# One level of the gated scores in a hybrid decoder layer: 16 by 16 products and ScalarE copies, or one product with 128 fixed columns and a masked copy

## The chip, the cores and the metric

The kernel runs on one core of one Trainium2 chip. The metric is the device time of one execution in microseconds (us). The core has TensorE for matrix products (its results land in PSUM), VectorE and ScalarE for elementwise work and for bringing results out of PSUM, GpSimd for further elementwise work, and SyncE, which issues most DMA transfers.

## The reference

One layer of a decoder runs for a prompt of 2048 tokens and for 8 samples of 8 tokens, with the same weights. After a norm comes one input projection; its columns feed four retention heads and four gated heads (HGRN2), all with 128 keys and 128 values. Their outputs are normed, gated, projected and added to the input; a squared-ReLU feed-forward layer follows. The part that matters here is the score matrix of the gated heads:

```python
def step(S, inp):                                  # one chunk of tokens
    qb, kb, vb, gb = inp                           # gb = log of the forget gate
    b = jnp.cumsum(gb, axis=2)
    diff = b[:, :, :, None, :] - b[:, :, None, :, :]
    decay = jnp.exp(jnp.where(causal[:, :, None], diff, -jnp.inf))
    A = jnp.einsum('bhtd,bhsd,bhtsd->bhts', qb, kb, decay)
    o = jnp.einsum('bhts,bhsv->bhtv', A, vb) + jnp.einsum('bhtd,bhdv->bhtv', qb * jnp.exp(b), S)
    ...
```

The decay between two tokens differs for each of the 128 key channels, so `A` is not one plain product of queries and keys.

## The kernel before, in words

The 2112 tokens are cut into three token groups: 640 prompt tokens, 768 prompt tokens, and 64 sample tokens with the last 640 prompt tokens. The kernel first does the mixing of each group (input projection, heads, output projection), then the feed-forward layer of each. Weights are streamed from memory; ScalarE and VectorE cut each into two parts, `hi` and `lo` (lines 273 and 287), and a projection multiplies three combinations of parts. These long runs of matmuls (`proj`, line 344; `values`, line 751; line 1214 in the feed-forward layer) make up most of the stream of TensorE.

**Order of the work.** `proj` and `values` call `tick()` as they go: in `proj` once for each weight and part, that is after two matmuls (one for each half of the tokens). Small work of the heads is hung on an agenda with `at(tick, function)`, and is emitted when the tick comes, so it stands between the matmuls of the projection of the next head. `mixer` fills the agenda for one head pair; ticks in this text are counted from its start. The order of emission is the order on TensorE; on the other engines the framework may move an instruction that it takes to be waiting behind others.

**The levels.** A chunk has C = 128 tokens. Its 128 by 128 score matrix, kept transposed (keys by queries) in `AT`, is put together by levels: for w in `LEVELS = (64, 32, 16, 8, 4, 2)` the tokens are cut into blocks of 2w, and the level gives the scores of the second w queries of each block with its first w keys. `exponents`, `decays` and `decayed` make a slab `x["qk", w]`, in which the first half of each block holds keys times the decay up to the middle of the block and the second half holds queries times the decay from there. A product of the two halves is then the wanted score. Level w = 16 is the one of 32 tokens.

A group has five or six chunks, split into two segments `g.segs`: two and three chunks in the first and the third group, three and three in the second. A level is done once for each segment `sg`, in one of three ways, chosen in `level` (line 1015):
- `kept` (line 911): for each chunk one matmul with the whole chunk, 128 columns, as fixed operand (weights) and all second halves, 64 columns, as moving operand (line 923). The result holds scores of all keys; VectorE's masked copy (`copy_predicated`, line 924) brings the wanted ones into `AT`.
- `corners` (line 971): for each chunk and each block one matmul with w fixed and w moving columns (line 980). ScalarE copies the results to their place in `AT`, one copy for each block position and all chunks of the segment (line 983).
- `quad` (line 999): the last level in another way.

All matmuls on `qk` are in fp32. Results go to PSUM banks of a pool of four, `pm` (tiles named `mm` and `po`), which all small work of the heads shares.

**Other work near this level.** `turn` (ticks 60 and 64 for the two segments) transposes keys on TensorE (line 853), and ScalarE brings them out (855 or 857). `own` (ticks 67 and 70) makes the diagonal of `AT` by sums over channels (lines 512 and 513) and a masked copy (944). `gates` and `project` take the finished projections out of PSUM (650) and apply the sigmoid on ScalarE (364, with a table load; the table for exponentials is loaded back at 366). Level w = 32 comes at ticks 52 and 55, level w = 8 at 73 and 76, each before the edit. The outputs read `AT` only after all levels (line 1103).

Of the kernel before, what the change touches and what calls it, by code (L numbers as in the profile page):

```python
# [202 lines left out]
class Kernel:  # L203
# [5 lines left out]
    def at(self, when, fn, *a):  # L209
        heapq.heappush(self.agenda, (when, self.n_at, fn, a))  # L210
        self.n_at += 1
# [651 lines left out]
    def mixer(self, g, p, b, t0):  # L863
# [9 lines left out]
        at = lambda t, fn, *a: self.at(t0 + t, fn, *a)  # L873
# [37 lines left out]
        def kept(i, qk, sg):  # L911

            w = LEVELS[i]
            second = lambda t: t.rearrange("p (n h m) -> p n h m", h=2, m=w)[:, :, 1]
            if sg == 2:
                ps = self.mm(NS // 2).rearrange("p (n m) -> p n m", m=w)
                nc.tensor.matmul(ps, qk[:, :P], second(qk[:, :NS]), start=True, stop=True)
                nc.vector.copy_predicated(second(self.ATs[:, :NS]), second(msk[:, NLV + i, :NS]), ps)
                return
            seg, m = g.segs[sg], len(g.segs[sg])  # L920
            ps = self.mm(m * P // 2).rearrange("p (c n m) -> p c n m", c=m, m=w)
            for j, c in enumerate(seg):
                nc.tensor.matmul(ps[:, j], qk[:, cols[c]], second(qk[:, cols[c]]), start=True, stop=True)  # L923
            nc.vector.copy_predicated(self.AT[sg][:, :m].rearrange("p c (n h m) -> p c n h m", h=2, m=w)[:, :, :, 1],
                                      second(msk[:, i]).unsqueeze(1).to_broadcast([P, m, P // (2 * w), w]), ps)
# [45 lines left out]
        def corners(w, sg):  # L971

            nb = P // (2 * w)
            seg, m = g.segs[sg], len(g.segs[sg])
            qk = x["qk", w]
            ps = self.mm(m * nb * w)
            for j, c in enumerate(seg):
                for r in range(nb):
                    s0 = cols[c].start + 2 * w * r
                    nc.tensor.matmul(ps[0:w, (r * m + j) * w:(r * m + j + 1) * w], qk[:, s0:s0 + w], qk[:, s0 + w:s0 + 2 * w],  # L980
                                     start=True, stop=True)
            for r in range(nb):
                nc.scalar.copy(self.AT[sg][2 * w * r:2 * w * r + w, :m, 2 * w * r + w:2 * w * (r + 1)],
                               ps[0:w, r * m * w:(r + 1) * m * w].rearrange("p (c t) -> p c t", t=w))
# [14 lines left out]
        def quad(sg):  # L999
            seg, m = g.segs[sg], len(g.segs[sg])  # L1000
            a, e = self.seg_cols(g, seg)
            s0 = cols[seg[0]].start
            second = lambda t: t.rearrange("p (n h i) -> p n h i", h=2, i=2)[:, :, 1]
            ps = self.mm(e - a)
            self.column_sums(ps, x["quad_hi"][:, a:e], x["quad_lo"][:, a:e])
            p4 = ps.rearrange("p (n i j) -> p n i j", i=2, j=2)
            nb, nq = (s0 - a) // 4, P // 4
            for j, i in ((0, LEVELS.index(2)), (1, 0)):
                if nb:
                    nc.vector.copy_predicated(second(self.ATs[:, :NS]), second(msk[:, NLV + i, :NS]), p4[:, :nb, :, j])  # L1010
                for c in range(m):
                    nc.vector.copy_predicated(second(self.AT[sg][:, c]), second(msk[:, i]),
                                              p4[:, nb + c * nq:nb + (c + 1) * nq, :, j])

        def level(i, sg):
            w = LEVELS[i]
            if w == 2:
                quad(sg)
            elif w >= 32:
                corners(w, sg)  # L1020
            else:
                kept(i, x["qk", w], sg)
# [102 lines left out]
        step, late, chunk, wait = 13, 24, 7, 14  # L1125
# [10 lines left out]
        for i, w in enumerate(LEVELS):  # L1136
            t = 6 + step * i
            at(t, exponents, w)
            at(t + 8, decays, w)
            at(t + 11, decayed, w)  # L1140
            if w == 2:
                at(t + 16, quad_products)
                at(t + 20, quad_parts)
            for sg in (parts if 2 < w < SLEN else range(2)):
                at(t + late + 3 * sg + (wait if w == 2 else 9 if w >= 32 else 4), level, i, sg)
        for sg in parts:
            at(46 + 4 * sg, ret_scores, sg)
            at(60 + 4 * sg, turn, "ktr", rk, sg, C_KS)
# [1 line left out]
        t = 6 + step * len(LEVELS)  # L1150
# [680 lines left out]
```

## Time and profile before

| | |
|---|---|
| median of 3 runs | 2495.11 us (2494.9 to 2495.3) |
| the profiled execution | 2495.74 us; its span from first to last instruction 2493.9 us |
| granted TensorE clock | 0.999 of full speed |
| matmul records on TensorE | 16536 |
| DMA | 525.67 MB, mean 211 GB/s |

In the lines of the profile PE is TensorE's matmul and PEld its weight load, DVE is VectorE, ACT is ScalarE, POOL is GpSimd; L923 is line 923 of the kernel. In a group of instructions the first numbers are the count, the busy time and the mean duration of one in ns; after the second bar stand the idle time before them and what ended it. A row of the chain of waits has the start in us, the length in us, and the line with the number of records that are merged in it.

### The profile page before, as it was taken

What the parts mean: (1) busy time and instruction counts of PE and PEld (TensorE: products, weight loads), DVE (VectorE), ACT (ScalarE), POOL (GpSimd) and SP (SyncE); (2) the same over time, 40 slices, a digit from 0 to 9 for tenths busy, and PEclk for the clock granted to TensorE, in tenths of its full rate; (3) what the DMA queues carried; (4) which work ended last, traced back from release to release, by engine and by line L of the source; (5) the groups of instructions that cost most, each with busy time, mean ns of one, the idle gap of its engine ahead of it and who ended that gap; (6) DMA issues with size and microseconds to landing.
All of it is one profiled execution on the core that took longest, in us unless ns stands there. A gap on an engine that the chain in (4) does not pass through costs nothing.

```text
span 2493.9 us, 41450 instructions
## 1 busy us (share of the span) xinstructions
PE 2480.4 (99%) x16536; PEld 2463.2 (99%) x16536; DVE 1876.4 (75%) x2453; ACT 1246.3 (50%) x1674; POOL 372.5 (15%) x312
## 2 busy tenths in 40 slices
PE   9999999999999999999999999999999999999998
PEld 9999999999999999999999999999999999999998
DVE  7666866667685767686875899776699878778987
ACT  6666663444454444453644554544454436445544
POOL 5223304324411442340000000000000000000000
PEclk9999999999999999999999999999999999999999
DMA  7444575465566665767866856576675545867552
GB/s 261 174 179 176 200 257 182 161 228 186 182 212 237 220 216 203 266 211 261 283 219 213 285 195 213 179 235 226 199 262 179 189 150 191 287 197 245 195 189 89
DMA packets 191655, 525.67 MB, mean 211 GB/s; under 512 B 20963, under 2 KB 62435, under 8 KB 191462
## 3 DMA queue, kind: packets, MB, share of 16 engines
q1 hardware_dynamic: 191318, 523.01, 61.3%
q8 instruction: 130, 2.13, 0.3%
q14 instruction: 63, 0.52, 0.1%
q10 hardware_dynamic: 144, 0.02, 0.0%
HBM read 389.51 MB, written 132.39 MB: 209 GB/s over the span
## 4 chain that ended last, share of the span: by engine, by line
PE 98%; DVE 1%; ACT 0%; DMA 0%; issue 0%; SPq 0%; DVEq 0%
PE pj L344 29%; PE pf L1214 26%; PE pj L1214 25%; PE pjv L751 8%; PE mm L923 2%; PE mm L1111 1%; PE po L1103 1%; PE po L1105 1%; PE mm L980 1%; PE mm L513 1%; PE mm L512 1%; PE po L787 1%; PE mm L1037 1%; PE mm L853 1%; DMA slab<-x 0%; ACT slab L549 0%
## 5 line engine op out<-in xcount | busy, mean ns | idle before, releaser
L273 ACT CAST hi<-raw 128x1024 fp32r<-128x1024 f32 x392 | 411.8, 1050 | 615.2 <-PE pf L1214 262.0
L344 PE MATMUL pj<-slab,hi 128*128 128x320 f32 (+2 forms) x3072 | 661.6, 328 | 2.9 <-DVE slab L650 1.0
L1214 PE MATMUL pf<-slab,hi 128*128 128x320 f32 (+2 forms) x2768 | 657.7, 321 | 0.0
L1214 PE MATMUL pj<-slab,hi 128*128 128x352 f32 (+2 forms) x2608 | 620.7, 322 | 0.0
L287 DVE TENSOR_TENSOR lo<-raw,hi 128x1024 fp32r<-128x1024 f32 x392 | 486.0, 1240 | 113.5 <-ACT hi L273 108.2
L344 PEld LDWEIGHTS pj<-slab,hi 128*128 128x128 f32 x3072 | 508.1, 188 | 5.5 <-DVE slab L650 1.3
L1214 PEld LDWEIGHTS pf<-slab,hi 128*128 128x128 f32 x2768 | 480.3, 188 | 0.0
L1214 PEld LDWEIGHTS pj<-slab,hi 128*128 128x128 f32 x2608 | 453.1, 188 | 0.1
L1214 PE MATMUL pf<-slab,lo 128*128 128x320 f32 (+2 forms) x1384 | 444.1, 321 | 0.0
L1214 PE MATMUL pj<-slab,lo 128*128 128x352 f32 (+2 forms) x1304 | 419.2, 321 | 0.0
L344 PE MATMUL pj<-slab,lo 128*128 128x320 f32 (+2 forms) x1536 | 379.5, 327 | 0.6 <-DVE lo L287 0.6
L344 PEld LDWEIGHTS pj<-slab,lo 128*128 128x128 f32 x1536 | 263.7, 188 | 1.8 <-DVE lo L287 1.1
L1214 PEld LDWEIGHTS pf<-slab,lo 128*128 128x128 f32 x1384 | 259.6, 188 | 0.0
L1214 PEld LDWEIGHTS pj<-slab,lo 128*128 128x128 f32 x1304 | 244.6, 188 | 0.0
L751 PE MATMUL pjv<-hi,slab 128*128 128x256 f32 (+1 forms) x1056 | 199.4, 285 | 0.0
L1305 ACT CAST slab<-slab 128x640 fp32r<-128x640 f32 (+2 forms) x192 | 145.3, 778 | 64.1 <-DVE slab L1316 51.7
L1309 DVE TENSOR_TENSOR slab<-slab 128x640 fp32r<-128x640 f32 (+2 forms) x192 | 167.3, 886 | 8.4 <-PE pj L1214 2.8
L751 PEld LDWEIGHTS pjv<-hi,slab 128*128 128x128 f32 (+1 forms) x1056 | 166.3, 190 | 1.4
L751 PE MATMUL pjv<-lo,slab 128*128 128x256 f32 (+1 forms) x528 | 149.2, 283 | 0.0
L902 ACT ACTIVATE slab<-slab 128x640 f32<-128x640 f32 (+2 forms) x72 | 56.3, 782 | 153.8 <-POOL slab L898 153.5
L751 PEld LDWEIGHTS pjv<-lo,slab 128*128 128x128 f32 (+1 forms) x528 | 100.3, 190 | 0.0
L1559 DVE TENSOR_TENSOR slab<-pf,slab 128x640 f32<-128x640 f32 (+2 forms) x88 | 77.6, 888 | 29.6 <-PE pf L1214 29.2
(222 smaller groups left out, 3000.5 us busy)
## 6 DMA issues: line engine op xcount, KB each, us to landing
raw<-w SPq DMA_DIRECT2D x264, 512.0 KB, 4.2
slab<-u SPq DMA_DIRECT2D x32, 384.0 KB, 5.0
u<-ld SPq DMA_DIRECT2D x30, 384.0 KB, 4.3
slab<-u SPq DMA_DIRECT2D x32, 352.0 KB, 4.8
u<-ld SPq DMA_DIRECT2D x30, 352.0 KB, 3.9
slab<-u SPq DMA_DIRECT2D x32, 320.0 KB, 4.5
u<-ld SPq DMA_DIRECT2D x30, 320.0 KB, 3.9
ld<-x SPq DMA_DIRECT2D x16, 384.0 KB, 3.7
```

The source lines that it names most:

```text
L273: self.nc.scalar.copy(hi, raw)
L287: self.nc.vector.tensor_tensor(out=lo, in0=self.second.pop(j), in1=hi.bitcast(F32), op=ALU.subtract)
L344: self.nc.tensor.matmul(pj[:, i, :T2], w, a[:, c0:c1], start=j == 0 and q == 0, stop=j == n - 1 and q == 2)
L512: self.nc.tensor.matmul(ps, self.ones_r, hi, start=True, stop=False)
L513: self.nc.tensor.matmul(ps, self.ones_r, lo, start=False, stop=True)
L751: nc.tensor.matmul(pj[:m, i * 256:(i + 1) * 256], a[:, s:s + m], ww, start=kb == 0 and q == 0, stop=m == C and kb == KB - 1 and q == 2, sk ...
L902: nc.scalar.activation(x["dd", w][:, a:T], x["dd", w][:, a:T], AF.Exp)
L923: nc.tensor.matmul(ps[:, j], qk[:, cols[c]], second(qk[:, cols[c]]), start=True, stop=True)
L1214: self.nc.tensor.matmul(*a, **k)
L1305: self.nc.scalar.copy(hi[:, :g.T], B[name][:, :g.T])
L1309: self.nc.vector.tensor_tensor(out=lo[:, :g.T], in0=B[name][:, :g.T], in1=hi.bitcast(F32)[:, :g.T], op=ALU.subtract)
L1559: nc.vector.tensor_tensor(out=r, in0=ps, in1=r, op=ALU.add)
```

## The change

Level w = 16 is done by `corners` and no longer by `kept`, and it is put at five ticks later, as the other `corners` levels are:

```diff
@@ level
             if w == 2:
                 quad(sg)
-            elif w >= 32:
+            elif w >= 16:
                 corners(w, sg)
             else:
                 kept(i, x["qk", w], sg)
@@ mixer
             for sg in (parts if 2 < w < SLEN else range(2)):
-                at(t + late + 3 * sg + (wait if w == 2 else 9 if w >= 32 else 4), level, i, sg)
+                at(t + late + 3 * sg + (wait if w == 2 else 9 if w >= 16 else 4), level, i, sg)
```

For each chunk one matmul of 128 fixed and 64 moving columns becomes four of 16 and 16. For each segment one masked copy on VectorE becomes four copies on ScalarE, each of 16 partitions. The level moves from ticks 60 and 63 to 65 and 68. The sample tokens take no part in this level, since their sequences have only 8 tokens.

## The prediction

> **What bounds the kernel now.** I read the page's busy table and the shares of its chain first, then who TensorE waited for, then its groups of instructions with shapes kept apart, and last the chain of waits in order of time around the edited step.
>
> ```profile
> PE 2480.4 (99%) x16536; PEld 2463.2 (99%) x16536; DVE 1876.4 (75%) x2453; ACT 1246.3 (50%) x1674; POOL 372.5 (15%) x312
> PE 98%; DVE 1%; ACT 0%; DMA 0%; issue 0%; SPq 0%; DVEq 0%
> ```
>
> TensorE is 98% of the chain that ended last. A high busy share alone would not show that it has no slack, so the next view is what its weight loads waited for (total us, times, longest us):
>
> ```profile
> PEld mm L980 <- issue: 4.3, 20, 0.3
> PEld pj L344 <- DVE slab L650: 1.3, 1, 1.3
> ```
>
> The longest total has no other engine behind it, and the next is one wait of 1.3 us. So VectorE and ScalarE practically never make TensorE wait; their work is free as long as that stays so, and a change is worth what it does to TensorE's own stream. That is what I price. The two kinds of step that the edit exchanges, as groups with shapes (busy us, mean ns of one record):
>
> ```profile
> L923 PE MATMUL mm<-slab 128*128 128x64 f32 x384 | 50.6, 264 | 0.0
> L980 PE MATMUL mm<-slab 128*32 128x32 f32 x256 | 12.6, 198 | 0.0
> ```
>
> Each fp32 matmul leaves two records, which I call passes: L923 is issued 3 levels x 16 chunks x 4 heads = 192 times and shows 384. The mean of 264 or 198 ns is the time until one is done, not the time that it takes from the stream, because they overlap. That time I read from the chain, which has no gaps: the start of one small group to the start of the next, less the projection matmuls (L344) between them.
>
> ```profile
> 132.30 0.37 PE mm L980 x8
> 132.67 1.08 PE pj L344 x6
> 133.74 0.49 PE mm L980 x12
> 134.24 1.66 PE pj L344 x10
> 135.90 0.39 PE mm L923 x4
> 136.29 0.23 PE mm L853 x2
> 136.51 0.88 PE pj L344 x6
> 137.39 0.61 PE mm L923 x6
> 138.00 0.35 PE pj L344 x2
> 138.35 0.33 PE mm L853 x3
> 138.68 0.87 PE pj L344 x6
> 139.55 0.12 PE mm L512
> ...
> 141.90 0.39 PE mm L923 x4
> 142.29 0.93 PE pj L344 x6
> 143.22 0.61 PE mm L923 x6
> 143.84 2.98 PE pj L344 x20
> 146.82 0.39 PE mm L923 x4
> ```
>
> This is a head of the first token group. The 32-token level that changes is the L923 pair at 135.90 (two chunks) and 137.39 (three chunks); the L980 pair ahead of it is the level of 64 tokens, already block by block; the pair at 141.90 is the next level, unchanged. An L344 matmul takes (2.98 - 0.93) / 14 = 0.146 us. Then:
> - old step, 2 chunks (4 passes): 143.22 - 141.90 - 6 x 0.146 = 0.44 us; 3 chunks (6 passes): 146.82 - 143.22 - 20 x 0.146 = 0.67 us. So 0.112 us a pass and nothing besides.
> - block by block with 32 columns, 2 chunks (8 passes): 133.74 - 132.30 - 0.88 = 0.56 us; 3 chunks (12 passes): 135.90 - 133.74 - 1.46 = 0.70 us. So 0.033 us a pass and a fixed 0.29 us for each group.
>
> The same for the level of 128 tokens, with 64 columns:
>
> ```profile
> 123.97 1.80 PE pjv L751 x15
> 125.76 0.38 PE mm L980 x4
> 126.14 0.55 PE pjv L751 x3
> 126.69 0.59 PE pj L344 x4
> 127.28 0.49 PE mm L980 x6
> 127.77 1.37 PE pj L344 x8
> 129.14 0.44 PE mm L1037 x4
> ```
>
> With L751 at 1.80 / 15 = 0.12 us: 4 passes take 126.69 - 125.76 - 0.36 = 0.57 us, 6 passes 129.14 - 127.28 - 8 x 0.146 = 0.69 us. So 0.06 us a pass and 0.33 us fixed. Narrower blocks have cheaper passes, but leaving and re-entering the 128-column form costs about 0.3 us each time, and the old step does not pay that.
>
> **The change part by part.** There are 24 groups, two for each of 4 heads in 3 token groups: 8 of two chunks (the first half in token groups 0 and 2) and 16 of three.
>
> *Removed from TensorE:* 8 x 0.44 + 16 x 0.67 = 14.2 us.
>
> *Added to TensorE:* four 16 by 16 products to a chunk, so 16 passes for two chunks and 24 for three: 8 x 16 + 16 x 24 = 512 passes, and 24 fixed costs. No row shows a 16-column pass. The price fell 112, 60, 33 ns at 128, 64, 32 columns, by 52 and then 27; halving the step again gives 20 ns, the lower bound. The upper bound is the nearest row itself, 33 ns, if a pass stops getting cheaper. I take 26 ns, the middle: the fall slows with each step, and one more full halving is the best case. The fixed part went 0.33, 0.29; I take 0.28 us, with 0.25 to 0.30 as its bounds. Added: 512 x 0.026 + 24 x 0.28 = 13.3 + 6.7 = 20.0 us.
>
> The Trainium skill (TensorE: Matmul & The Clock Gate, section "Wait — 56ns, not 53.3ns?") says that the spacing of matmul starts does not fall below about 25 ns however few columns there are. By that page the sum would be 512 x 0.025 + 6.7 = 19.5 us, half a microsecond less. No row of this trace is narrow enough to show it: the 33 ns rows lie above it.
>
> *Moved:* the level goes from ticks 60 and 63 to 65 and 68. At tick 60 it stood directly ahead of the key transposes (L853 at 136.29). The two together took 137.39 - 135.90 - 0.88 = 0.61 us. Transposes alone of three take 139.55 - 138.35 - 0.88 = 0.32 us, at one more pass of 0.11 than two, so two alone take 0.21 us. Apart they cost 0.44 + 0.21 = 0.65 us, so separating them costs 0.04 us in each of 12 heads: 0.5 us. The key transposes, the own products (L512, L513) and the next level keep their ticks, and no DMA moves.
>
> *VectorE and ScalarE* (groups with shapes, then the mixing stage by windows, then ScalarE in order of time):
>
> ```profile
> L924 DVE COPY_PREDICATED AT<-msk,mm 128x192 f32<-128x192 uint8 x48 | 17.5, 366 | 20.0 <-PE mm L923 13.6 <-issue 4.2 <-ACT slab L902 1.5
> L983 ACT COPY AT<-mm 32x96 f32<-32x96 f32 x32 | 7.2, 224 | 8.2 <-PE mm L980 7.9
> L983 ACT COPY AT<-mm 32x64 f32<-32x64 f32 x16 | 3.2, 200 | 13.5 <-PE mm L980 7.7 <-DVE AT L967 5.7
> 40.00:1130.00 1090.00, 1088.19 (x7809) 1074.52 (x7808) 760.83 (x1204) 552.43 (x843) 353.89 (x294) 1.00 0.58 205
> 138.72 0.58 ACT L857 ACTIVATE slab<-mm,con 128x384 f32<-128x384 f32 x1 [0.24 <-PE mm L853]
> 139.31 1.28 ACT L364 ACT_TABLE_LOAD   x1
> 140.61 0.74 ACT L364 ACTIVATE slab<-slab 128x640 f32<-128x640 f32 x1
> 141.37 1.28 ACT L366 ACT_TABLE_LOAD   x1
> ```
>
> VectorE loses 24 masked copies of at most 0.37 us, under 9 us of its 761 in the 1090 us stage. ScalarE gains 96 copies; their block is smaller than that of the 0.20 and 0.22 us rows, so about 0.2 us each, 19 us on top of 552. Neither bounds this stage, so I cost both at nothing for now; what hides them is TensorE's own stream. Behind the waiting copies on ScalarE stand the weight casts, the exponentials and the sigmoid's table loads, and the own products' masked copies on VectorE now follow them on the same tile. The cover is gone if a PSUM bank is then not free in time. The small groups share four banks, and the group that takes this level's first bank again is the next level's at 141.90. In this head ScalarE may reach the first copies only when the table loads end, 141.37 + 1.28 = 142.65, and leave them 4 x 0.2 later at 143.45. TensorE comes there later than 141.90 by the two new groups, 0.28 + 16 x 0.026 = 0.70 us and 0.90 us: 143.5. (What leaves the stream ahead of both shifts both alike.) So the bank is free just as it is wanted: no wait, but no margin.
>
> *Sum:* 20.0 - 14.2 + 0.5 = +6.3 us on TensorE's stream, which is the span. The profiled execution took 2495.74 us (span 2493.9 and 1.8 around it) and should take 2502.0; its distance of 0.6 to the median of 2495.11 is no part of this, so the median should be 2501.4.
>
> A measurement of this kernel can tell about 0.2%, 5.0 us. In general the change is 512 x pass + 24 x fixed - 13.7 us; with 0.28 us fixed it reaches 5.0 us at a pass of 23.4 ns and zero at 13.7 ns.
>
> **The rivals.**
> *The pass keeps falling (other side, not slower).* If it is 20 ns, the change is 10.2 + 6.7 - 13.7 = +3.2 us, 2498.3 us; it decides below 23.4 ns. For it: three measured widths fall nearly in proportion. Against it: something fixed must remain in each pass, and the step per halving already shrinks. Faster by 0.2% would need 4 ns a pass, or the fixed part gone as well as a pass near 20 ns; both L980 widths pay it, so I give that almost nothing.
>
> *The pass stops falling.* At 33 ns and 0.29 us fixed: 16.9 + 7.0 - 13.7 = +10.2 us, 2505.3 us. For it: the nearest row; against it: nothing in the trace shows the end of the fall. The Trainium skill (TensorEngine Tiling (Array Packing), section "Instruction Overhead") says a matmul with one column takes as long as one with 60. By that rule 16 columns cost what 32 cost, and the trace agrees only in part, since 64 to 32 columns still fell by 27 ns.
>
> *ScalarE becomes late.* If one exponential (0.74 us) or the like stands ahead of the copies, TensorE waits that long for the bank: in the four heads of the first token group 3 us, so 2504.4 us; in all twelve 9 us, 2510. For it: the missing margin above. Against it: TensorE waited for no bank so far, and the table loads stand at this point only where a projection block ends near tick 65.
>
> *It does not do what it says:* if a 16-column product is run in the 128-column form, the fixed 0.28 us goes, and at 20 to 26 ns the change is -3.5 to -0.4 us, 2491.6 to 2494.7 us, within the measurement.
>
> **How the numbers follow.** Forecast (pass of 23.4 to 30 ns, no new wait) 0.45; pass still falling 0.27; pass as at 32 columns 0.15; late ScalarE 0.10; the 128-column form 0.03. Slower by over 0.2%: 0.45 + 0.15 + 0.10, less a little for a fixed part at its lower bound, 0.68. Within 0.2%: 0.30. Faster: 0.02. The likeliest case gives 2501.4. The range runs from 2497.3 (20 ns with 0.25 us fixed, 2497.6, and a little under it) to 2506.8 (33 ns and half of the four heads' wait); outside lie the 128-column form and the longer waits.
>
> **What would show it.** In the changed profile L923 falls to 256 records and L980 gains 512 of a 16-column form; the chain shows x16 and x24 groups of L980, each with 0.28 us more than its passes. The difference of a x24 and a x16 group, divided by 8, is the disputed price: 26 ns, or 20, or 33. L983 gains 96 copies of about 0.2 us. Waits of TensorE for ScalarE or VectorE copies inside the mixing stage would show the third rival. The forecast is wrong if the L980 groups of 16 columns come without the fixed part, or if the feed-forward stage, which the edit does not touch, changes its length.

## The result, and the profile after

The changed kernel takes 2503.39 us (median of 6 runs, 2502.16 to 2506.07), the kernel before 2495.20 us beside it: ratio 1.0031, 95% interval 1.0021 to 1.0041. It is 8.2 us slower; the forecast was 6.3 us. The profiled execution has a span of 2501.0 us, 7.1 us more than before, with the same granted clock of 0.999. Single runs of the kernel before fall into two groups nearly 2 us apart (2494.4 to 2495.4 us and 2496.3 to 2497.2 us in the 31 runs beside the first four experiments), so a median can move by that much with no change to the kernel.

From the page, TensorE's line of the busy table and the shares of the chain:

```profile
PE 2485.9 (99%) x16920; PEld 2462.4 (98%) x16920; DVE 1867.1 (75%) x2429; ACT 1262.5 (50%) x1770; POOL 370.7 (15%) x312
PE 97%; DVE 1%; ACT 1%; DMA 1%; issue 0%; SPq 0%; DVEq 0%; ACTq 0%
```

The 384 further records of TensorE are 512 passes more and 128 fewer; VectorE has 24 instructions fewer, ScalarE 96 more. As groups with shapes kept apart:

```profile
L923 PE MATMUL mm<-slab 128*128 128x64 f32 x256 | 34.0, 265 | 0.2 <-ACT AT L983 0.2
L980 PE MATMUL mm<-slab 128*16 128x16 f32 x512 | 16.8, 177 | 0.0
L983 ACT COPY AT<-mm 16x48 f32<-16x48 f32 x64 | 12.0, 187 | 7.5 <-PE mm L980 6.8
```

The price of the new groups, from the chain of waits in order of time, in the head that the prediction used (start us, length us, line, records):

```profile
138.49 0.49 PE mm L980 x16
138.99 0.77 PE pj L344 x4
139.76 0.12 PE mm L512
...
140.30 0.69 PE mm L980 x24
140.99 0.79 PE pj L344 x4
141.78 0.18 PE mm L512
...
142.13 1.61 PE pj L344 x11
143.75 0.39 PE mm L923 x4
144.14 0.20 PE pj L344
144.34 0.65 PE mm L923 x6
```

With 0.146 us for an L344, two chunks cost 139.76 - 138.49 - 0.58 = 0.69 us and three 141.78 - 140.30 - 0.58 = 0.90 us. The difference over 8 passes gives 0.026 us a pass, and 0.28 us fixed. (From the same records at the resolution of 1 ns, medians of the groups: 0.691 and 0.893 us, so 25.2 ns a pass and 0.29 us.) The last four rows show the next level. Its ticks did not change, but its first group now comes after 11 L344 matmuls and not after 6, and it splits a pair of them: the framework placed it later. So on TensorE, too, the order of emission is not always the order of execution.

What TensorE's weight loads waited for:

```profile
PEld mm L980 <- issue: 8.4, 38, 0.3
PEld pj L344 <- DVE slab L650: 2.0, 1, 2.0
...
PEld mm L923 <- ACT AT L983: 0.7, 2, 0.5
PEld po L784 <- DVE slab L814: 0.6, 1, 0.6
```

The first line is the entry into the narrow form, 38 times and not 20. The wait for L650 was 1.3 us and is 2.0 us; the last two are new.

### The profile page after: what moved, and what is told of

It reads as the page before. It is cut to its first block, busy times and chain, and to the rows that moved or that the text cites. A ratio compares the mean times of both kernels' runs of the same rounds, so it can differ in the third digit from the quotient of the medians.

```text
span 2501.0 us, 42289 instructions
## 1 busy us (share of the span) xinstructions
PE 2485.9 (99%) x16920; PEld 2462.4 (98%) x16920; DVE 1867.1 (75%) x2429; ACT 1262.5 (50%) x1770; POOL 370.7 (15%) x312
## 4 chain that ended last, share of the span: by engine, by line
PE 97%; DVE 1%; ACT 1%; DMA 1%; issue 0%; SPq 0%; DVEq 0%; ACTq 0%
PE pj L344 29%; PE pf L1214 26%; PE pj L1214 25%; PE pjv L751 8%; PE mm L980 1%; PE mm L1111 1%; PE po L1103 1%; PE po L1105 1%; PE mm L923 1%; PE mm L513 1%; PE mm L512 1%; PE po L787 1%; PE mm L1037 1%; PE mm L853 1%; DMA ld<-x 0%; ACT slab L549 0%
## 5 line engine op out<-in xcount | busy, mean ns | idle before, releaser
L344 PE MATMUL pj<-slab,hi 128*128 128x320 f32 (+2 forms) x3072 | 661.7, 328 | 4.0 <-DVE slab L650 1.8
L344 PEld LDWEIGHTS pj<-slab,hi 128*128 128x128 f32 x3072 | 508.4, 188 | 6.5 <-DVE slab L650 2.0
L344 PE MATMUL pj<-slab,lo 128*128 128x320 f32 (+2 forms) x1536 | 381.2, 328 | 0.5 <-DVE lo L287 0.4
L344 PEld LDWEIGHTS pj<-slab,lo 128*128 128x128 f32 x1536 | 263.4, 188 | 2.2 <-DVE lo L287 1.0
```

Of the source, the lines that this page charges most:

```text
L344: self.nc.tensor.matmul(pj[:, i, :T2], w, a[:, c0:c1], start=j == 0 and q == 0, stop=j == n - 1 and q == 2)
```

## The experiments

All are compared with the kernel before, run beside them on the same chip. The differences are of some 0.1% to 0.4%, and medians of one kernel on different chips differ by about 1 us, so the prices come from the profiles and the medians are the check. The diffs below are shortened to the expressions that change.

**The place alone.** The old step at the new ticks:

```diff
-  (wait if w == 2 else 9 if w >= 32 else 4)      # level w = 16 stays with kept()
+  (wait if w == 2 else 9 if w >= 16 else 4)
```

> The old step (one product of 128 fixed columns, VectorE's masked copy) at the new ticks 65 and 68. Theory (the loss is TensorE's stream: passes and the fixed part of each group): only the separation from the key transposes is paid, +0.5 us, so about 2495.7 us, ratio 1.0002. Rival (the later place makes other work late or sets off waits, and this is the 1 to 2 us that the group prices of the changed kernel do not cover): +1.5 to +2.5 us, 2496.7 to 2497.7.

2496.96 us against 2496.30, ratio 1.0003 (0.9994 to 1.0011). The interval reaches from 1.5 us less to 2.7 us more, so the times can't tell the expected 0.5 us from the rival's 2 us. The profile says more. Its wait for L650 is 1.2 us, as before the change, but one of the two new waits is there, although neither the form nor ScalarE's copies changed:

```profile
PEld po L784 <- DVE slab L814: 0.5, 1, 0.5
```

So this wait comes with the place. The span is 2494.1 us, 0.2 us above that of the kernel before, and L1037 of the first head, a product of the retention heads ahead of the moved level, starts at 54.57 us here and at 55.53 us before. Counted from there the place costs about 1.2 us: this wait, and near to what the prediction gave the separation.

**The form alone.** `corners` for w = 16, at the old ticks 60 and 63:

```diff
-  elif w >= 32:                                  # ticks as before
+  elif w >= 16:
```

> The 16 by 16 products and ScalarE's copies at the old ticks 60 and 63. Theory (stream): 512 passes of 25 ns and 24 fixed parts of 0.29 us for 14.2 us, +5.6 us, 2500.8 us; the x24 and x16 groups cost 0.89 and 0.69 us as in the changed kernel. Rival (place and waits matter): differs from the changed kernel's +8.2 us by more than 1 us beside these prices, or shows waits of TensorE for ScalarE's copies of 1 us and more in the mixing stage.

2502.71 us, +6.4 us, ratio 1.0024 (1.0015 to 1.0034). The group of three chunks costs the same again. In the chain of waits:

```profile
137.31 0.69 PE mm L980 x24
138.00 0.50 PE pj L344 x2
138.50 0.33 PE mm L853 x3
```

138.50 - 137.31 - 0.29 = 0.90 us. Most of the loss comes with the form. The changed kernel had lost 1.8 us more by the medians, and the expectation had named a distance above 1 us as a sign that the place matters too. The waits of L923 and L784 are missing from this profile, so these two come only with the new place; the wait for L650 is here without it (1.9 us).

**VectorE brings the results out.**

```diff
-  nc.scalar.copy(self.AT[sg][...], ...)
+  (nc.vector.tensor_copy if w == 16 else nc.scalar.copy)(self.AT[sg][...], ...)
```

> The changed kernel with the 16-column results brought out by VectorE (four plain copies a segment) and not by ScalarE. Theory (stream): TensorE's groups are unchanged, +6 to +7 us, 2501.2 to 2502.2 us. Rival (ScalarE is late): its 19 us of copies cause what the group prices leave over, so this one is 2 us faster than the changed kernel and the two new waits of TensorE near the ends of heads (0.56 and 0.75 us) are gone; if it is as slow or slower, ScalarE's copies are not the cause.

2502.34 us, +6.0 us, ratio 1.0023 (1.0014 to 1.0032). TensorE's groups are the same, but its wait at the end of the mixing is as short as before the change:

```profile
PEld pj L344 <- DVE slab L650: 1.3, 1, 1.3
```

Both expectations come to about +6 us, so the time does not decide between them; the waits do. The wait for L650 is back at its old length and that of L923 is gone, so ScalarE's copies do cost something, beside the stream. The wait of L784 fell to 0.3 us and did not go.

**ScalarE's copies in one head only.** As the change, but VectorE brings the results out in the last head of the third token group:

```diff
+  nc.vector.tensor_copy if w == 16 and n0 and p == H - 1 else nc.scalar.copy
```

> The changed kernel with VectorE bringing out the 16-column results in the last head of the third token group only; ScalarE does the other eleven heads as in the change. Theory (what the group prices leave over comes from ScalarE's 8 copies in that one head, which make the work after them 1 us later, so that TensorE waits 2.0 us and not 1.3 us at the end of the mixing): that wait is back at 1.3 us, and the median is +6 to +7 us, without the executions at +10 us. Rival (the copies of all heads add up): the wait stays at 2.0 us and the median at +8 us.

2502.64 us against 2495.07, +7.6 us, ratio 1.0030 (1.0019 to 1.0042), highest run 2503.45. The median lies between the two expectations. The wait for L650 is 1.3 us, so this one head decides it. ScalarE in order of time there, first in the changed kernel, then with VectorE's copies:

```profile
1106.75 0.57 ACT L857 ACTIVATE slab<-mm,con 128x384 f32<-128x384 f32 x1
1107.22 1.53 ACT L983 COPY AT<-mm 16x32 f32<-16x32 f32 x8
1108.77 0.47 ACT L816 ACTIVATE slab<-mm,con 96x256 fp32r<-96x256 f32 x1
```

```profile
1106.12 0.57 ACT L857 ACTIVATE slab<-mm,con 128x384 f32<-128x384 f32 x1
1107.37 0.47 ACT L816 ACTIVATE slab<-mm,con 96x256 fp32r<-96x256 f32 x1 [0.67 <-PE mm L810]
```

Eight copies, 1.53 us, stand ahead of the sample keys (L816). Without them L816 starts 1.25 us after the start of L857, with them 2.02 us: 0.77 us later, which is about the growth of TensorE's wait for L650 from 1.3 to 2.0 us some 20 us on. VectorE passes it on: it takes up the sample keys (L817), and later waits for the sigmoid of this head (L364), first in the changed kernel, then with VectorE's copies:

```profile
1109.28 0.48 DVE L817 SCALAR_TENSOR_TENSOR slab<-mm,con,slab 32x256 fp32r<-32x256 f32 x1 [0.85 <-ACT slab L816]
1116.98 0.95 DVE L672 SCALAR_TENSOR_TENSOR slab<-slab,vec 128x704 f32<-128x704 f32 x1 [1.03 <-ACT slab L364]
```

```profile
1107.88 0.48 DVE L817 SCALAR_TENSOR_TENSOR slab<-mm,con,slab 32x256 fp32r<-32x256 f32 x1
1115.59 0.95 DVE L672 SCALAR_TENSOR_TENSOR slab<-slab,vec 128x704 f32<-128x704 f32 x1 [0.26 <-ACT slab L364]
```

The distance from L817 to L672 is 7.70 us in one and 7.71 us in the other, so the delay is there at L817 and is passed on from it. The wait for L650 comes once in the whole profile. The median moved by less than the scatter of medians, so the 0.7 us are shown by the two profiles and not by the times.

**One visit for both segments.** `corners` multiplies both segments at the second one's tick, into one PSUM bank:

```diff
-  ps = self.mm(m * nb * w)                       # once for each segment
+  ps = self.mm(sum(m for both segments) * nb * w)
```

> The changed kernel with both segments of the 16-column level in one visit at the second segment's tick, in one PSUM bank: the same 512 passes in 12 groups and not 24. Theory (the fixed part is paid once for each visit): 12 x 0.29 = 3.4 us less than the changed kernel, +4.8 us by its median and +2.8 us by the stream alone, 2498.0 to 2500.0 us. Rival (the fixed part belongs to the chunks or to the wait for the copies): no difference, 2503.4 us.

2500.95 us, +4.7 us, ratio 1.0019 (1.0010 to 1.0028). From its chain:

```profile
138.23 1.09 PE mm L983 x40
139.33 0.78 PE pj L344 x4
140.11 0.17 PE mm L512
```

40 passes cost 140.11 - 138.23 - 0.58 = 1.30 us, where the two visits took 0.69 + 0.90 = 1.59 us. The fixed 0.29 us is paid for each visit; 12 of them are 3.5 us, and the medians (+8.2 and +4.7 us) differ by as much.

**Twice the passes.** Each product as two with 8 moving columns:

```diff
+  for h in (0, 8):
-  matmul(ps[...], qk[:, s0:s0 + w], qk[:, s0 + w:s0 + 2 * w])
+  matmul(ps[... + h], qk[:, s0:s0 + w], qk[:, s0 + w + h:s0 + w + h + 8])
```

> The changed kernel with each 16 by 16 product done as two products of 16 fixed and 8 moving columns: twice the passes, the same result. Theory (a pass does not get cheaper than about 25 ns): the x24 group becomes x48 and costs 0.29 + 48 x 0.025 = 1.49 us, 0.60 us more, and the span grows by 512 x 0.025 = 12.9 us. Rival (the 25 ns of 16 columns was only the next value of a falling price): passes of 18 to 20 ns, a x48 group of 1.15 to 1.25 us, and 6 to 8 us on the span.

One run, 2513.78 us; span 2512.0, 11.0 us above the changed kernel's. The chain:

```profile
138.19 0.89 PE mm L982 x32
139.08 0.78 PE pj L344 x4
139.87 0.12 PE mm L512
...
140.40 1.29 PE mm L982 x48
141.69 0.78 PE pj L344 x4
142.47 0.18 PE mm L512
```

32 passes cost 139.87 - 138.19 - 0.58 = 1.10 us, 48 passes 142.47 - 140.40 - 0.58 = 1.49 us: 0.025 us a pass and 0.29 us fixed. Halving the moving columns saved nothing. (The groups alone make 12.8 us. The span grew by 11.0 only: the wait of L923 for a bank, 0.7 us, is missing here, that for L650 is 1.7 and not 2.0 us, and the same L1037 (L1039 in this kernel), ahead of all edited groups, starts at 54.42 and not at 54.99 us. These make 1.6 us.) The fixed 16 columns stayed, so a floor for the load of still fewer fixed columns is not shown by this.

**Fewer visits, without and with the change.** If a visit costs 0.29 to 0.33 us, the two levels that were block by block already pay too much. The first kernel leaves the level of 32 tokens as before, and does w = 64 and w = 32 in one visit each (at the second segments' ticks); it was run twice:

```diff
-  for sg in range(2): at(t + late + 3 * sg + 9, level, i, sg)
+  at(t + late + 12, level, i, 0)                 # both segments in one bank
```

> The kernel before, with the levels of 128 and 64 tokens (64 and 32 columns) done for both segments in one visit each; the level of 32 tokens as before the change. Theory (the fixed part is paid once for each visit of TensorE to a narrower form): 12 x 0.33 + 12 x 0.29 = 7.4 us less than before, ratio 0.9970. Rival (the fixed part grows with the chunks, or what is saved comes back as waits for four more copies at once): less than 3 us.

> The kernel before with one visit for the 64-column and one for the 32-column level, again, beside the last one on the same chip. Theory (stream): -7.4 to -8.2 us as the first time; the all-block version should be 0.5 to 1.5 us faster than it, if its waits are gone. Rival: no difference between the two.

2487.68 us both times: -8.6 us (ratio 0.9967, 0.9954 to 0.9979) and -7.4 us (0.9971, 0.9960 to 0.9982). The next kernel does w = 16 block by block too, in the same visit as w = 32, with VectorE's copies; the one after puts w = 64 into that visit as well:

```diff
+  for when, vs in ((45, (64,)), (62, (32, 16))): # then: ((62, (64, 32, 16)),)
+      for v in vs: at(when, level, LEVELS.index(v), 0)
```

> All three levels block by block; both segments in one visit; the 32 and 16 column levels in the same visit, back to back at tick 62; the 16-column results brought out by VectorE. Theory (within a visit a further narrow level pays only its passes): 64 columns -4.0, 32 columns -3.5, 16 columns 512 x 0.025 - 14.2 = -1.3, separation +0.5, together -8.3 us against before, ratio 0.9967, so the change of form itself gains 1.3 us once nothing fixed is paid for it. Rival (each level pays its own fixed part even back to back): 12 x 0.28 = 3.4 us more, -4.9 us.

> As the last one, with the 64-column level in the same visit too (tick 62, before the 32 and 16 columns). Theory: the 12 fixed parts of the 64-column visits go, -4.0 us more, -12.3 us against before, ratio 0.9951. Rival (going from 64 to 32 columns is itself such a switch, as leaving the 128-column form is): no more than the last one, -8.3 us.

The two visits: 2489.19 us, -7.1 us (0.9974, 0.9964 to 0.9985), between the two expectations and nearer to the theory's -8.3 us. Its chain in one head of the first group, and a wait of its weight loads:

```profile
133.26 1.74 PE mm L983 x60
135.00 0.77 PE pj L344 x4
135.77 0.33 PE mm L853 x3
```

```profile
PEld mm L810 <- ACT AT L989: 1.9, 4, 0.9
```

20 passes of 32 columns and 40 of 16 cost 135.77 - 133.26 - 0.58 = 1.93 us. By the prices 20 x 0.033 + 40 x 0.025 + 0.29 = 1.95 us: between 32 and 16 columns nothing fixed is paid. The 1.9 us of waits are for ScalarE's copies of the 32-column results to free a bank. The single visit of all three was worse, 2491.67 us (0.9983, 0.9974 to 0.9991), with longer waits:

```profile
PEld mm L853 <- ACT slab L857: 3.2, 4, 1.8
...
PEld mm L983 <- DVE slab L1045: 2.1, 3, 1.7
```

So neither expectation was met there: it gained 4.6 us, and 12.3 or 8.3 us were expected. These two waits are 5.3 us, more than the 4.0 us that the fewer visits should save; that they come from three banks at once is argued and not shown.

**The best version** is the one with two visits, with the 32-column results brought out by VectorE too:

```diff
-  (nc.vector.tensor_copy if w == 16 else nc.scalar.copy)
+  (nc.vector.tensor_copy if w < 64 else nc.scalar.copy)
```

> The kernel with all three levels block by block in two visits, with the results of 32 columns brought out by VectorE too. In its predecessor TensorE waited 1.9 us in four places for ScalarE's copies of the 32-column results to free a bank. Theory: these waits go and nothing else changes, 1.9 us less, -8.5 us against before or somewhat more. Rival (VectorE then becomes late): as slow as the predecessor, -6.5 us.

2485.67 us (2485.57 to 2487.27) against 2495.07, -9.4 us, ratio 0.9963 (0.9951 to 0.9976). Its profile has no wait of L810 left. Beside it the version that keeps the masked copy took 2487.68 us (2486.99 to 2489.82); the intervals of the two ratios overlap, and the 2 us between them are larger than the 0.5 to 1.5 us that were expected. The spans of the two profiles, 2483.8 and 2485.9 us, are as far apart. It beats both kernels of this case, and in it the changed form does no harm.

**The changed kernel again.**

> The changed kernel once more, beside the three below. Theory (TensorE's stream): the group prices of its first profile give +6.2 us, and the medians of single chips scatter by about 1 us around that, so +5.5 to +8.2 us. Rival (ScalarE's copies add 2 us of waits every time): +8.2 us again.

2506.06 us against 2496.28, +9.8 us; ratio 1.0035 (1.0022 to 1.0048), more than either expectation. Here the profiled execution had a span of 2504.5 us, 3.5 us over the first one, and by windows (busy us of PE, PEld, DVE, ACT, POOL, then granted clock) this:

```profile
1128.00:1134.00 6.00, 5.10 (x27) 5.10 (x28) 6.00 (x19) 3.08 (x5) 0.99 (x1) 0.72 0.27 80
1129.64:1133.05 3.41, 3.41 (x17) 3.41 (x16) 3.41 (x11) 2.32 (x5) 0.04 (x1) 0.50 0.00 0
```

In the 6 us after the wait for L650, again 2.0 us long, the clock was granted at 0.72 on average, and at 0.50 for 3.41 us of them. The first profile has the same wait with a clock of 1.00 in these 6 us. By the starts of the same records in both, this stretch makes 1.5 of the 3.5 us, and 0.4 us lie ahead of the first edited group. The rest comes in the feed-forward stage, between about 2100 and 2230 us, with the clock at 1.00. There 96 matmuls took this long, in the first profile and in this one:

```profile
2153.17 15.25 PE pf L1214 x96
```

```profile
2155.76 15.47 PE pf L1214 x96
```

Over the stretch that is 1.7 us. Six of the fourteen profiles have the longer form: this one, the form alone, VectorE's copies, the copies in one head, the one visit and the two visits. Both forms are found for the changed kernel, so this is not the edit; its cause is open. It means that 1.7 of the 2.9 us between the spans of the two-visit kernel (2486.7 us) and the best version (2483.8 us) are not the work of VectorE's copies.

## Why the prediction was right

**TensorE's stream.** This carried the forecast, and its terms held. Removed: 14.2 us, not disputed by any run. Added: a pass of 25 ns where 26 was taken, a fixed part of 0.29 us where 0.28 was taken; 512 x 0.0252 + 24 x 0.29 = 19.9 us where 20.0 was forecast. The single pass price lay between the two rivals, and both fell: 20 ns did not come, nor 33. The sentence of the Trainium skill (TensorE: Matmul & The Clock Gate, section "Wait — 56ns, not 53.3ns?"), with its floor of about 25 ns, was the better source than the middle of two bounds; the products of 8 columns agree with it at 25 ns. That 26 ns came so close was luck, since nothing but two bounds stood behind it. The Trainium skill (TensorEngine Tiling (Array Packing), section "Instruction Overhead") says that 1 to 60 columns take the same time; 16 and 8 moving columns agree with it at 25 ns. The 33 ns of 32 columns do not test it, since there the fixed columns are 32 too.

**The separation.** It was put at 0.5 us. The times of the run with the place alone can't tell this from nothing; its profile bears it out, but shows a further cost of the place that the prediction does not have, the wait of L784 (0.5 us there, 0.6 us in the changed kernel).

**ScalarE's copies.** The prediction cost them at nothing and named the missing margin of the banks as a rival with 0.10. This is the step that was mis-sized, in two places. In the first head of the first token group it went as the rival says: ScalarE reached the copies only after the sigmoid's table loads, and the next level waited for its bank. From the chain of the changed kernel:

```profile
67.19 1.28 ACT L366
...
68.49 0.17 ACT AT L983
...
69.27 0.66 PE mm L923 x4
```

This cost 0.7 us, once and not four times: in the next head, the one that the prediction worked out, the framework put the next level later. What the prediction did not see is the last head of the mixing, where TensorE already waited 1.3 us for VectorE: there 1.53 us of copies ahead of the sample keys became 0.7 us more of that wait, 20 us later.

**The sum.** New groups and separation less the old ones are 6.2 us. The new waits (0.7 us for banks, 0.7 at L650, 0.6 at L784) make 2.0 us on top of the stream, 8.2 us together, against 7.1 us on the span. Half of the difference lies ahead of the edited step, where the changed kernel's profile was early by chance; in the first head, before and after the change:

```profile
55.53 0.45 PE mm L1037 x4
```

```profile
54.99 0.44 PE mm L1037 x4
```

So from there on the kernel lost 7.6 us; the other 0.6 us are not traced. That the stream alone gives 6.2 us where the forecast was 6.3 is the forecast borne out; that the median came to the same 8.2 us as the sum with the waits is chance, as the next paragraph shows.

**The median** is another 1 us above the span. Two things that differ from one execution to the next move it: the 1.7 us of the feed-forward stage, and the clock after the longer wait. The one run at 2506 us that was profiled (2506.30 us) has both. The granted clock is listed as 0.998 for all four runs above 2506 us and one of 2503.96 us, and as 0.999 for the other six of this kernel, so the clock probably fell in those too. With the wait at 1.3 us (the two runs with VectorE's copies) no run of 16 was above 2503.5 us, and none is listed below 0.999.

**What the prediction named as signs** came as named: 256 records of L923, 512 of the narrow form, groups of 16 and 24 with their fixed part, and, in the first profile, a feed-forward stage that did not change. (The 1.7 us there in the second profile are not the edit's, as said above.)

## What to carry to other kernels

Where TensorE is the bound, price a small group from start to start in the chain of waits, not by the duration of its matmuls: cutting a product into small blocks pays a fixed price for each visit to the narrow form, and below some width a pass gets no cheaper. So collect the small products of several levels and segments into one visit before making them smaller. And look for the places where the covering work runs out; a wait that is there already shows one. A microsecond on another engine that costs nothing in ten heads can be a wait in the first and in the last one.

## What the runs showed of the hardware that was not expected

Going from 32 to 16 columns within one visit cost nothing (1.93 us measured, 1.95 us from the passes and one fixed part), while going from 128 to either costs 0.29 us. After a wait of TensorE of 2.0 us the granted clock was 0.50 for 3.41 us in one execution, and 1.00 in another with the same wait; in the kernel with one visit for both segments it was 0.50 for 3.41 us too, after a wait of 2.2 us. The Trainium skill (TensorE: Matmul & The Clock Gate, section "What's actually happening") gives 3.4 us as the length of a window of the gate and half speed for its throttled state, and says that the window is free-running; the rows agree with the length and the speed, and two executions with the same wait and different clocks fit the last point.
